# S5 parameter batches of a two-layer encoder: double-buffered tables, fetched two batches ahead on the GpSimd queue

## The chip, the cores and the metric

The kernel runs on one core of a Trainium2 chip. The metric is the device time of one execution in microseconds (us); the time of before is the median of three runs. Engines are named as the profile names them: PE (TensorE), DVE (VectorE), ACT (ScalarE), POOL (GpSimd), SP (SyncE, which here only issues transfers). Each engine works through its own list of instructions in order.

## The reference, cut to what matters

Two layers over 256 tokens of width 2048, all in float32. Layer 0 mixes tokens with sparse latent attention and an RWKV7 recurrence, layer 1 with a complex diagonal state space, S5. Behind each mixer come a cross-attention to a memory and a feed-forward block of width 8192 with squared ReLU.

```python
def s5_mixer(u, lam_re, lam_im, log_dt, b_re, b_im, c_re, c_im, d_skip, w_glu, b_glu):
    ...
    lam_bar = jnp.exp(lam * dt)
    b_bar = ((lam_bar - 1.0) / lam)[..., None] * lax.complex(b_re.astype(f32), b_im.astype(f32))
    c_mat = lax.complex(c_re.astype(f32), c_im.astype(f32))
    ...                       # scan of x <- lam_bar x + b_bar u;  y = Re(C x) + d u, gelu, gate

def squared_relu_mlp(xn, w_up, w_down):
    return jnp.square(jax.nn.relu(xn @ w_up)) @ w_down
```

## The kernel before

Everything is kept transposed, features on partitions and tokens along the free axis. A weight matrix comes in half chunks of [128, 1024] (512 KB): `w_load` (L228) issues the load on SP into a tile `st`, and `w_split` makes of each half of it an exact pair, `whi` (a copy on ACT, L236) and `wlo` (a subtraction on DVE, L238), so that three matmuls (L302 to L304, the third with `wlo`) give the product in full precision. `whi` and `wlo` have a few buffers each: PE runs some quarters of a chunk behind ACT and DVE, and stops when `wlo` is late.

The stage around the change is the feed-forward block of layer 0, `ffn(0, ...)`. It has 64 `up` and 64 `down` units of 48 matmuls each; `mm3` uses four `whi`/`wlo` pairs of 512 columns per unit. After each unit one step of another stream is recorded, `S5Params.steps()`, which prepares layer 1: it turns the parameters of the state space alone into matrices and leaves them in DRAM.

- `base()` makes powers of the state matrix (`pw`), a complex factor `f`, and a table by token, which it stores to the DRAM tile `tokens` (L1333).
- `batch(m)`, m = 0 to 15, has six steps. Step 0 loads `bc` (128 KB, two buffers), `bT` (512 KB) and `tT` (512 KB, from `tokens`), the last two in one buffer each; DVE forms `bb` = `bc`·`f` by `cmul` (six instructions, L1294 to L1299) and ACT copies it into `bd` (L1384, L1385). Step 1: `cmul` of `bT` and `tT` to `bt`. Step 2: `cmul` of `bc` and `pw` to `cl`. Step 3: ACT turns `cl` into `co`; stores `rec2<-co` (L1401) and `rec1<-bt` (L1402). Step 4: 8 small matmuls (L1407) of `bd` and `cl`, copied to `tt`. Step 5: store `rec2<-tt` (L1414).
- `phases()` makes tables `E` on POOL alone: 18 instructions for `u`, then four quarters of 52 instructions, each followed by four stores `rec1<-E` (L1363). All POOL instructions here are recorded at L211, through a wrapper that keeps them in the order in which they are written; `cmul` is shared, so its lines are L1294 to L1299 on DVE. `E` has one buffer, so a quarter begins when the stores of the last one have landed.

`mix1`, after the stage, reads all `rec` tiles back. A scheduler in the tile framework sets the order of each engine's list when the kernel is built; waits follow from the tiles and their buffers. So where an instruction stands in its engine's list is fixed before the kernel runs.

Of the kernel before, what the change touches and what calls it, by code (L numbers as in the profile page):

```python
# [6 lines left out]
F32 = mybir.dt.float32  # L7
# [13 lines left out]
def _tile_weight(w):  # L21
    """[K, M] -> chunks [n, 128, 2048]: per chunk (m-tile, k-tile, column)."""
    K, M = w.shape
    kt, mt = K // P, M // P
    t = w.reshape(kt, P, mt, P).transpose(2, 1, 0, 3)
    per = 2048 // (kt * P)
    t = t.reshape(mt // per, per, P, kt, P).transpose(0, 2, 1, 3, 4)
    return np.ascontiguousarray(t).reshape(mt // per, P, 2048)
# [17 lines left out]
def _consts():  # L46
    """Tables that depend on the shapes alone."""
# [34 lines left out]
def layout(inp):  # L82
# [53 lines left out]
    # features of 8 groups per tile, the channel of a group before the group  # L136
    fo = np.arange(D).reshape(KT, 8, 16).transpose(0, 2, 1).reshape(-1)
    out['win1'] = _tile_weight(inp['odd_w_in'][0][:, fo])
    # past the state space: group bits (1, 0), group bit 2, channel
# [5 lines left out]
    # states on partitions: (group of the pair, state); pairs of groups along the free axis  # L145
# [13 lines left out]
# steps of the streams in the first layer per step of a pair of heads  # L159
# [12 lines left out]
def build(tc, a, parts=('mix0', 'x0', 'f0', 'mix1', 'x1', 'f1')):  # L172
# [5 lines left out]
    with ExitStack() as es:  # L178
# [26 lines left out]
        class InOrder:  # L205
            """An engine whose instructions stay behind all that was issued on it before."""
# [24 lines left out]
        def w_split(st, i, half):  # L231
            """half of a half chunk as an exact pair hi + lo of float32r"""
# [9 lines left out]
        # columns of 512 whose low parts GpSimd takes from VectorE  # L242
# [6 lines left out]
        class Feed:  # L249
            """Half chunks of weights in order, loaded ahead of their use on their own buffers;  # L250
            split ahead of it too, in quarters of a chunk."""
# [23 lines left out]
            def done(self, q=None):  # L275
                """quarter q (the current one) has been used"""
# [5 lines left out]
        class chunk:  # L282
            """1 MiB of weights, split in quarters."""
# [22 lines left out]
        def units(w_ap, xs, evac, kt=16):  # L306
            """All output tiles of a weight; evac(m, psum)."""
# [8 lines left out]
        def mm_k(ps, w, at, x, first, last):  # L316
            """one K tile of an output tile, in three exact float32r products"""
# [6 lines left out]
        def units_g(feed, n, xs, evac, bank, kt=16, grain=4, m0=0, pre=None):  # L324
            """n output tiles of kt products each, a few products per step. pre: steps to take
            between the first products and the first evacuation."""
# [24 lines left out]
        def split(pool_, name, x, scale=None):  # L351
            """x (times a column) as an exact pair of float32r tiles."""
# [10 lines left out]
        def rnorm_g(ring, sq, ind, scale, eps, floor=False):  # L363
            """1/sqrt(scale * sum over a group of features + eps) per token and group,
            as PSUM [128 features, 256 tokens]. The tiles sq hold squares, ind the groups [128, n]."""
# [22 lines left out]
        class Norm:  # L388
            """x * gain, tile by tile, as f32r pairs or in place; 1/rms per token comes later, on the products."""
# [51 lines left out]
        # ---- residual, transposed: [feature, token]  # L441
# [9 lines left out]
        # ---- memory keys and values (do not depend on x)  # L451
# [41 lines left out]
        def soft(sp, nk, bias=None, scale=1.0, ring=tmp):  # L493
            """softmax over the free axis of scores [128, nk]; returns an SBUF tile."""
# [97 lines left out]
        def reduced_sincos(pool_, name, ang, k, y, shape, e=V):  # L592
            """cos and sin of ang, brought to -pi..pi first"""
# [32 lines left out]
        def rope_g(ring, dst, x, cs, perm, rows):  # L626
            """dst = x * cos + (perm x) * sin on the first rows; x in SBUF."""
# [10 lines left out]
        def begin():  # L638
            """Loads x; the first output tiles of the three streams of weights side by side."""
# [22 lines left out]
            def products(i, q):  # L662
                """a quarter of an output tile"""
# [18 lines left out]
        def mix0(nxt):  # L682
# [10 lines left out]
            def load_y(p, y, ys):  # L693
                """mixed heads, back from DRAM and split"""
# [7 lines left out]
            with ExitStack() as right:  # L702
                with ExitStack() as left:
# [7 lines left out]
                    def shifted(pool_, name, ps, i, p0=0, p1=P):  # L711
                        """h + (shift(h) - h) * mu for one tile of features."""
# [43 lines left out]
                    def paced(key, s):  # L756
                        """the steps of a stream that fall to one step of a pair"""
# [41 lines left out]
        class DSA:  # L799
            """Sparse latent attention; everything transposed, [feature, token]."""  # L800
            def __init__(self, n, r0, dp, ya):
# [6 lines left out]
                # the values' tile, free for now, as scratch  # L808
# [792 lines left out]
```

## Time and profile before

| | us |
|---|---|
| median of three runs (lowest, highest) | 2735.43 (2733.37, 2742.15) |
| span of the profiled execution | 2736.0 |
| PE busy | 2608.3 (95%) |
| DVE busy | 1942.3 (71%) |
| ACT busy | 1356.8 (50%) |
| POOL busy | 588.3 (22%) |

The profiled execution has a span of 2736.0 us from its first instruction to its last; no other time of its own is recorded, and it lies 0.6 us above the median of the runs. Busy times overlap, so their sum says nothing; PE is busy nearly always, and what the kernel can win lies in the stretches in which it is not.

### The profile page before, as it was taken

The numbers are of one execution on the slowest core, as the hardware profiler recorded it, in microseconds if no ns is written. First come the engines' busy times: TensorE is split into PE (matmuls) and PEld (weight loads), VectorE is DVE, ScalarE is ACT, GpSimd is POOL, SyncE is SP. The second block draws the span as 40 slices with busy tenths as digits, with TensorE's granted clock in tenths as the row PEclk, the third lists the DMA queues.
The fourth block names the chain that finished last, engine by engine and source line by source line (L and its number), as shares of the span: only waits on it lengthen the run. The fifth ranks groups of instructions, "written<-read, shape, count | busy, mean of one in ns | idle before, by whom it ended". The sixth has DMA issues, their size and how long they took to land.

```text
span 2736.0 us, 57870 instructions
## 1 busy us (share of the span) xinstructions
PE 2608.3 (95%) x22078; PEld 2500.9 (91%) x22078; DVE 1942.3 (71%) x4202; ACT 1356.8 (50%) x2860; POOL 588.3 (22%) x860
## 2 busy tenths in 40 slices
PE   7889999999998999999999998999999999999997
PEld 7877888789898899999999998999999999999997
DVE  6678878757878777777766798566766656666565
ACT  4444445335654455455465545555554454454553
POOL 5344435436686000000000223001400000000001
PEclk9999999899999999999999999999999999999998
DMA  5323344244367777777766586555355555555553
GB/s 195 122 96 112 113 155 153 91 128 168 140 199 250 246 228 235 243 235 230 240 223 242 195 311 232 185 186 190 142 181 183 186 184 185 185 185 186 182 184 136
DMA packets 184038, 510.40 MB, mean 187 GB/s; under 512 B 41808, under 2 KB 66640, under 8 KB 181712
## 3 DMA queue, kind: packets, MB, share of 16 engines
q1 hardware_dynamic: 182704, 504.47, 54.6%
q8 instruction: 173, 2.83, 0.4%
q0 software_dynamic: 768, 2.10, 0.2%
q14 instruction: 105, 0.86, 0.1%
q10 hardware_dynamic: 288, 0.14, 0.0%
HBM read 472.55 MB, written 34.09 MB: 185 GB/s over the span
## 4 chain that ended last, share of the span: by engine, by line
PE 68%; DVE 16%; DMA 8%; issue 4%; ACT 2%; POOL 1%; SPq 0%; DVEq 0%; ACTq 0%; POOLq 0%
PE acc L304 16%; PE acc L302 16%; PE acc L303 16%; DVE wlo L238 5%; PE acc L320 5%; PE acc L321 4%; PE acc L322 4%; DMA tT<-tokens 4%; DMA bc<-s5bc 2%; ACT whi L236 1%; PE ms L1115 1%; DMA st<-up 1%; DMA st<-wA 1%; DVE t L1145 1%; PE ms L1098 1%
## 5 line engine op out<-in xcount | busy, mean ns | idle before, releaser
L238 DVE TENSOR_TENSOR wlo<-st,whi 128x512 fp32r<-128x512 f32 (+3 forms) x1568 | 1058.9, 683 | 541.8 <-ACT whi L236 530.8
L236 ACT CAST whi<-st 128x512 fp32r<-128x512 f32 x1568 | 949.2, 621 | 958.6 <-PE acc L303 462.9
L304 PE MATMUL acc<-hh,wlo 128*128 128x256 f32 x2048 | 582.5, 284 | 16.7 <-DVE wlo L238 16.7
L302 PE MATMUL acc<-hh,whi 128*128 128x256 f32 x2048 | 579.8, 283 | 3.1 <-ACT whi L236 2.5
L303 PE MATMUL acc<-hl,whi 128*128 128x256 f32 x2048 | 578.4, 282 | 0.1
L304 PEld LDWEIGHTS acc<-hh,wlo 128*128 128x128 f32 x2048 | 387.9, 189 | 22.8 <-DVE wlo L238 22.2
L302 PEld LDWEIGHTS acc<-hh,whi 128*128 128x128 f32 x2048 | 387.9, 189 | 5.9 <-ACT whi L236 3.9
L303 PEld LDWEIGHTS acc<-hl,whi 128*128 128x128 f32 x2048 | 387.8, 189 | 0.3 <-DVE hl L357 0.3
L409 POOL TENSOR_TENSOR xnsq<-xnsq,t 128x256 f32<-128x256 f32 x125 | 106.0, 848 | 1105.6 <-PE acc L304 798.3
L240 POOL TENSOR_TENSOR wlo<-st,whi 128x192 fp32r<-128x192 f32 (+2 forms) x274 | 205.7, 758 | 284.5 <-ACT whi L236 216.0
L1438 POOL MEMSET S<- 128x512 f32 x2 | 1.0, 521 | 499.3 <-ACT hh L356 499.3
L304 PE MATMUL acc<-zh,wlo 128*128 128x256 f32 x256 | 72.1, 282 | 0.0
L302 PE MATMUL acc<-zh,whi 128*128 128x256 f32 x256 | 72.0, 281 | 0.0
L303 PE MATMUL acc<-zl,whi 128*128 128x256 f32 x256 | 72.0, 281 | 0.0
L303 PE MATMUL acc<-ol,whi 128*128 128x256 f32 x256 | 71.5, 279 | 0.0
L302 PE MATMUL acc<-oh,whi 128*128 128x256 f32 x256 | 71.5, 279 | 0.0
L304 PE MATMUL acc<-oh,wlo 128*128 128x256 f32 x256 | 71.5, 279 | 0.0
L574 DVE TENSOR_TENSOR t<-acc,xnr 128x256 f32<-128x256 f32 x128 | 53.8, 421 | 20.1 <-PE acc L304 20.1
L356 ACT CAST hh<-t 128x256 fp32r<-128x256 f32 x128 | 51.8, 404 | 32.6 <-DVE t L566 32.2
L357 DVE TENSOR_TENSOR hl<-t,hh 128x256 fp32r<-128x256 f32 x128 | 55.2, 431 | 4.1 <-ACT hh L356 4.1
L575 DVE TENSOR_TENSOR x<-x,t 128x256 f32<-128x256 f32 x128 | 54.3, 424 | 3.6
L566 DVE SCALAR_TENSOR_TENSOR t<-acc,t 128x256 f32<-128x256 f32 x128 | 53.2, 415 | 0.2 <-ACT t L564 0.2
(788 smaller groups left out, 7788.8 us busy)
## 6 DMA issues: line engine op xcount, KB each, us to landing
st<-up SPq DMA_DIRECT2D x256, 512.0 KB, 3.4
st<-down SPq DMA_DIRECT2D x256, 512.0 KB, 3.7
st<-wout SPq DMA_DIRECT2D x64, 512.0 KB, 3.8
st<-wB SPq DMA_DIRECT2D x48, 512.0 KB, 4.0
st<-wkv SPq DMA_DIRECT2D x32, 512.0 KB, 4.0
R<-rec SPq DMA_DIRECT2D x16, 1024.0 KB, 7.5
st<-win SPq DMA_DIRECT2D x32, 512.0 KB, 3.7
st<-glu SPq DMA_DIRECT2D x32, 512.0 KB, 3.7
```

Of the source, the lines that this page charges most:

```text
L236: A.copy(hi, st)
L238: V.tensor_tensor(lo[:, :n], st[:, :n], hi[:, :n].bitcast(F32), OP.subtract)
L240: G.tensor_tensor(lo[:, n:], st[:, n:], hi[:, n:].bitcast(F32), OP.subtract)
L302: T.matmul(ps, hi, xh, start=k == 0, stop=False)
L303: T.matmul(ps, hi, xl, start=False, stop=False)
L304: T.matmul(ps, lo, xh, start=False, stop=k == nk - 1)
L320: T.matmul(ps, hi, xh, start=first, stop=False)
L321: T.matmul(ps, hi, xl, start=False, stop=False)
L322: T.matmul(ps, lo, xh, start=False, stop=last)
L357: V.tensor_tensor(l, x, h.bitcast(F32), OP.subtract)
L409: G.tensor_tensor(self.sq[0], self.sq[0], s, OP.add)
L575: V.tensor_tensor(xT[m], xT[m], t, OP.add)
```

## The change

The three loads of a batch move into `fetch(m)`, all with two buffers. `fetch(0)` and `fetch(1)` are recorded at the end of `base()`, `fetch(m + 2)` in step 2 of `batch(m)`. They are issued by POOL instead of SP, and so are the stores of `tokens`, `co`, `bt` and `tt`. The copies into `bd` are recorded in step 1, after the `cmul` of `bt`. Scratch tiles of `base()` share the buffers of `co`, `bt` and `cl`, since `bT` and `tT` are now taken by the fetches. Comments are gone too, so that lines shift. The arithmetic is as before.

```diff
-                pb = p.tile([P, 2, 64, 8], F32, name='pb')
+                pb = p.tile([P, 2, 64, 8], F32, name='pb', tag='cl')
-                tk = p.tile([P, 1024], F32, name='tT').rearrange('p (m s c g) -> p m s c g', m=16, s=8, c=2)
+                tk = p.tile([P, 1024], F32, name='tk', tag='co').rearrange('p (m s c g) -> p m s c g', m=16, s=8, c=2)
-                tq = p.tile([P, 1024], F32, name='bT').rearrange('p (a q) -> p a q', a=8)
+                tq = p.tile([P, 1024], F32, name='tq', tag='bt').rearrange('p (a q) -> p a q', a=8)
...
-                nc.sync.dma_start(tokens.rearrange('a (r q) -> r a q', r=P), tq)
+                nc.gpsimd.dma_start(tokens.rearrange('a (r q) -> r a q', r=P), tq)
...
+                self.got = {}
+                self.fetch(0)
+                self.fetch(1)
+                yield
+
+            def fetch(self, m):
+
+                if m >= 16:
+                    return
+                p = self.p
+                bc = p.tile([P, 4, 4, 16], F32, name='bc', bufs=2)
+                bT, tT = (p.tile([P, 1024], F32, name=nm, bufs=2) for nm in ('bT', 'tT'))
+                nc.gpsimd.dma_start(bc, a['s5bc'][m])
+                nc.gpsimd.dma_start(bT, a['s5bT'][m].unsqueeze(1).to_broadcast([16, 8, 1024]))
+                nc.gpsimd.dma_start(tT, tokens[m // 2].rearrange('(b s f) -> b s f', b=2, s=8)[m % 2].unsqueeze(0)
+                                    .to_broadcast([16, 8, 1024]))
+                self.got[m] = bc, bT, tT
...
-                bc = p.tile([P, 4, 4, 16], F32, name='bc', bufs=2)
-                nc.sync.dma_start(bc, a['s5bc'][m])
-                bT, tT = (p.tile([P, 1024], F32, name=nm) for nm in ('bT', 'tT'))
-                nc.sync.dma_start(bT, a['s5bT'][m].unsqueeze(1).to_broadcast([16, 8, 1024]))
-                nc.sync.dma_start(tT, tokens[m // 2].rearrange('(b s f) -> b s f', b=2, s=8)[m % 2].unsqueeze(0)
-                                  .to_broadcast([16, 8, 1024]))
+                bc, bT, tT = self.got.pop(m)
...
+                self.cmul((bt[:, :, 0], bt[:, :, 1]), x, y,
+                          t.rearrange('p a b c -> p (a b c)')[:, :512].rearrange('p (g q) -> p g q', g=4))
                 for h in range(2):
                     hs = slice(64 * h, 64 * h + 64)
                     A.copy(bd[hs, 0, :, h], bb[hs, 0])
                     A.activation(bd[hs, 1, :, h], bb[hs, 1], AF.Copy, scale=-1.0)
...
                           (each(self.pw[:, 0, g4], 9), each(self.pw[:, 1, g4], 9)), t)
+                self.fetch(m + 2)
                 yield
...
-                nc.sync.dma_start(rec2[m][:, 0:1024], co.rearrange('p a g o j -> p (a g o j)'))
-                nc.sync.dma_start(rec1[m][:, 0:1024], bt.rearrange('p g a q -> p (g a q)'))
+                nc.gpsimd.dma_start(rec2[m][:, 0:1024], co.rearrange('p a g o j -> p (a g o j)'))
+                nc.gpsimd.dma_start(rec1[m][:, 0:1024], bt.rearrange('p g a q -> p (g a q)'))
...
-                nc.sync.dma_start(rec2[m][:, 1024:2048].rearrange('(i s) (g f) -> g i s f', s=8, g=8),
+                nc.gpsimd.dma_start(rec2[m][:, 1024:2048].rearrange('(i s) (g f) -> g i s f', s=8, g=8),
```

On SP, around batches 6 and 7, each batch of before has six transfers between the weight loads, which are the rows L228 (`up`, `down`):

```order
L1373 DMA tT<-tokens 128x1x1024
L228 DMA st<-up 128x1024 x2
L228 DMA st<-down 128x1024 x4
L1414 DMA rec_5_108<-tt 8x128x128
L228 DMA st<-down 128x1024
L1370 DMA bc<-s5bc 128x256
L1401 DMA rec_6_109<-co 128x1024
L228 DMA st<-down 128x1024 x3
L1372 DMA bT<-s5bT 128x1x1024
L228 DMA st<-down 128x1024
```

After the change SP holds the weight loads of the stage and nothing else, from the first parameter load (`raw`) on:

```order
L228 DMA st<-up 128x1024
L1257 DMA raw<-s5lam 128x192
L228 DMA st<-up 128x1024 x35
L228 DMA st<-down 128x1024 x32
L228 DMA st<-up 128x1024 x32
```

All six transfers have left SP's list.

On POOL, at the beginning of `phases()`, the difference reads as follows; `xnsq` belongs to the norm ahead of the stage, and `ut` and `u` are the first instructions of `phases()`:

```order
 L409 TENSOR_TENSOR xnsq<-xnsq,t 128x256 x8
+L1333 DMA tokens<-tq 128x8x128
+L1350 DMA tT<-tokens 128x1x1024 x2
 L211 TENSOR_TENSOR ut<-scc,scs 128x64
-L211 TENSOR_TENSOR u_11220<-scs,scc 128x64
-L211 TENSOR_TENSOR u_11220<-u_11220,ut 128x64
+L211 TENSOR_TENSOR u_11222<-scs,scc 128x64
+L211 TENSOR_TENSOR u_11222<-u_11222,ut 128x64
```

The whole of `phases()` now stands behind the store of `tokens` and two loads of `tT`, which read what it wrote.

Further down POOL's list, at the end of the second quarter, before the change there are only `E` and its stores (this is the end of the first quarter, and the second ends alike):

```order
L211 TENSOR_TENSOR et<-E 128x16x15
L211 TENSOR_TENSOR E<-E 128x16x15
L211 TENSOR_TENSOR E<-E,et 128x16x15
L1363 DMA rec_0_86<-E 128x2x128
L1363 DMA rec_1_87<-E 128x2x128
L1363 DMA rec_2_88<-E 128x2x128
L1363 DMA rec_3_89<-E 128x2x128
L211 MEMSET E 128x16 x2
```

After it, at the end of the second quarter (the load of `bc` is that of batch 3):

```order
L211 TENSOR_TENSOR et<-E 128x16x15
L211 TENSOR_TENSOR E<-E 128x16x15
L211 TENSOR_TENSOR E<-E,et 128x16x15
L1379 DMA rec_4_90<-E 128x2x128
L1348 DMA bc<-s5bc 128x256
L1379 DMA rec_5_91<-E 128x2x128
L1379 DMA rec_6_92<-E 128x2x128
L1413 DMA rec_1_104<-co 128x1024
L1379 DMA rec_7_93<-E 128x2x128
L1349 DMA bT<-s5bT 128x1x1024
```

From the first `u` to the load of `bc` for batch 3, POOL now has the 18 instructions of `u`, two quarters of 52, and 14 transfers. The loads of `bc` for batches 4 and 5 stand behind 24 and 20 more instructions of `phases()` after the stores of `tt` of batches 1 and 2. The last 16 stand between the loads of batches 5 and 6; behind them POOL's list holds the transfers alone.

On DVE, where a batch gives its `bc` buffer back and the batch after next reads it again, before the change (batch 2 reads bc_12353 for the last time in the first row, and bc_13452 of batch 4 takes that buffer):

```order
L1297 TENSOR_TENSOR t9_12359<-bc_12353,pw_10199 128x576
L238 TENSOR_TENSOR wlo_12387<-st_12384,whi_12386 128x512
L1299 TENSOR_TENSOR cl_12546<-cl_12546,t9_12359 128x576
L574 TENSOR_TENSOR t_12259<-acc_12190,xnr2_10102 128x256
L238 TENSOR_TENSOR wlo_12403<-st_12384,whi_12402 128x512
L575 TENSOR_TENSOR x1_5223<-x1_5223,t_12259 128x256
L1294 TENSOR_TENSOR t9_12917<-bc_12911,f_10113 128x4x16
L238 TENSOR_TENSOR wlo_12421<-st_12418,whi_12420 128x512
L1296 TENSOR_TENSOR bb_12918<-bb_12918,t9_12917 128x64
L1295 TENSOR_TENSOR bb_13459<-bc_13452,f_10113 128x64
```

After it, the same place (bc_11438 of batch 2, bc_12559 of batch 4):

```order
L1297 TENSOR_TENSOR t9_12365<-bc_11438,pw_10199 128x576
L238 TENSOR_TENSOR wlo_12389<-st_12386,whi_12388 128x512
L1299 TENSOR_TENSOR cl_12552<-cl_12552,t9_12365 128x576
L574 TENSOR_TENSOR t_12271<-acc_12202,xnr2_10102 128x256
L238 TENSOR_TENSOR wlo_12405<-st_12386,whi_12404 128x512
L575 TENSOR_TENSOR x1_5223<-x1_5223,t_12271 128x256
L1294 TENSOR_TENSOR t9_12923<-bc_12001,f_10113 128x4x16
L1295 TENSOR_TENSOR bb_13465<-bc_12559,f_10113 128x64
```

The first use of the new `bc` stands 9 rows behind the last read of the old one before, 7 after; over the batches it is 9 or 10 before (but 50 and 32 in the first two), and 7, 10 or 13 after. For `bT` and `tT` the distance grows from 14 to 18 rows to 51 to 68, since each now has two buffers.

## Rows read from the trace of the kernel before

**Rows 1.** The page's head:

```profile
span 2736.0 us, 57870 instructions
```

**Rows 2.** Busy time by stretch: window, length, then each engine's busy us (instructions), PEclk, DMA share, GB/s:

```profile
820.00:1000.00 180.00, 165.16 (x1348) 159.04 (x1347) 139.22 (x257) 84.50 (x186) 47.67 (x86) 0.98 0.78 245
1000.00:1320.00 320.00, 303.31 (x2508) 294.52 (x2507) 231.05 (x456) 161.36 (x364) 0.00 (x0) 0.97 0.75 235
1990.00:2710.00 720.00, 718.11 (x6019) 717.91 (x6018) 440.95 (x767) 361.13 (x661) 8.85 (x12) 1.00 0.52 183
```

**Rows 3.** The same, of line L1407 alone (first PE):

```profile
820.00:1000.00 180.00, 2.67 (x64) 1.59 (x64) 0.98 0.78 245
1000.00:1320.00 320.00, 6.44 (x144) 3.83 (x144) 0.97 0.75 235
```

**Rows 4.** Waits of PE, 820 to 1320: us, times, longest:

```profile
PE acc L304 <- DVE wlo L238: 28.3, 34, 2.5
```

**Rows 5.** Waits of DVE, 820 to 1320:

```profile
DVE wlo L238 <- ACT whi L236: 61.3, 45, 4.5
DVE bb L1295 <- DMA bc<-s5bc: 22.0, 11, 3.1
DVE bt L1295 <- DMA tT<-tokens: 20.5, 7, 4.0
```

**Rows 6.** Waits of ACT, 820 to 1320:

```profile
ACT whi L236 <- DMA st<-down: 83.7, 43, 5.4
ACT bd L1384 <- DVE bb L1299: 24.6, 13, 3.0
```

**Rows 7.** Chain of waits, 1010 to 1062: start, us, what:

```profile
1016.23 6.49 DMA bc<-s5bc
...
1031.72 8.29 DMA tT<-tokens
```

**Rows 8.** The stores of E on POOL, L1363: issue duration, who waited, landing:

```profile
L1363 POOL DMA_DIRECT2D rec<-E x16: 723/723/949, 764.5 to 876.1; - x16
...
  POOL E L211: 12.5, 3
...
DMA to landing us min/median/max: 3.0/4.5/6.0
```

**Rows 9.** Order of time on POOL, 725 to 880: start, us, instruction:

```profile
729.15 0.36 POOL L211 TENSOR_TENSOR ut<-scc,scs 128x64 f32<-128x64 f32 x1 [1.66 <-ACT scc L616]
...
737.87 0.17 POOL L211 MEMSET E<- 128x16 f32 x2
...
764.55 3.12 POOL L1363 DMA_DIRECT2D rec<-E  x4 [0.30 <-POOL E L211]
770.53 0.17 POOL L211 MEMSET E<- 128x16 f32 x2 [2.86 <-DMA rec<-E]
...
802.52 2.93 POOL L1363 DMA_DIRECT2D rec<-E  x4 [0.30 <-POOL E L211]
...
811.32 0.25 POOL L211 TENSOR_TENSOR et<-E 128x16 f32<-128x16 f32 x1
...
816.09 0.71 POOL L211 TENSOR_TENSOR et<-E 128x16 f32<-128x16 f32 x1
```

**Rows 10.** Order of time on SP, 806 to 825:

```profile
808.03 0.43 SPq L1333 DMA_DIRECT2D tokens<-bT  x1
...
815.25 0.59 SPq L1373 DMA_DIRECT2D tT<-tokens  x1
```

**Rows 11.** Order of time on DVE, 820 to 870:

```profile
822.17 0.69 DVE L1294 TENSOR_TENSOR t<-bT,tT 128x512 f32<-128x512 f32 x1 [3.99 <-DMA tT<-tokens]
...
868.65 0.26 DVE L1294 TENSOR_TENSOR t<-bc,f 128x64 f32<-128x64 f32 x1
```

**Rows 12.** Waits of DVE, 868 to 984:

```profile
DVE bt L1295 <- issue: 8.6, 2, 5.1
DVE bb L1295 <- DMA bc<-s5bc: 5.1, 3, 2.7
DVE bt L1295 <- DMA tT<-tokens: 1.9, 1, 1.9
```

More of the change, by code (lines that the diff above doesn't have):

```diff
@@ L1381, in batch @@
                 bd = self.bd[m % 2]
-                for h in range(2):
-                    hs = slice(64 * h, 64 * h + 64)
-                    A.copy(bd[hs, 0, :, h], bb[hs, 0])
-                    A.activation(bd[hs, 1, :, h], bb[hs, 1], AF.Copy, scale=-1.0)
                 over = lambda ap, n: ap.unsqueeze(2).to_broadcast([P, 4, n, 16])
@@ L1392, in batch @@
                           t.rearrange('p a b c -> p (a b c)')[:, :512].rearrange('p (g q) -> p g q', g=4))
+                for h in range(2):
+                    hs = slice(64 * h, 64 * h + 64)
+                    A.copy(bd[hs, 0, :, h], bb[hs, 0])
+                    A.activation(bd[hs, 1, :, h], bb[hs, 1], AF.Copy, scale=-1.0)
                 yield
```

## The prediction

> **What bounds the kernel now.** I began with the page's head [rows 1] and then cut the span into stretches [rows 2], since the change acts only while `ffn(0)` runs beside the batches. The reader should compare matmuls per us. From 1990 to 2710, where the second feed-forward block runs alone, PE does 6019 matmuls in 720 us, 8.36 per us, at a granted clock of 1.00 (the 2.4 GHz level): nothing is missing there. From 820 to 1000 and from 1000 to 1320 it does fewer. What these stretches lose is their length, less their large matmuls at 8.36 per us, less what the batches' own matmuls take [rows 3]. Early: 180 − (1348 − 64)/8.36 − 2.67 = 23.7 us. Late: 320 − (2508 − 144)/8.36 − 6.44 = 30.8 us. So the batches cost 54.5 us beyond their PE work, and that is all a change of theirs can win.
>
> Then the waits, from PE backwards. PE waits on `wlo` of DVE [rows 4]; DVE waits for `whi` of ACT, and for the tables `bc` and `tT` [rows 5]; ACT waits for weight loads, and for `bb` before it can fill `bd` [rows 6]. The chain in the late part shows which of these end last: the landing of `bc` (6.49 us) and of `tT` (8.29) follow each other, with little between them but DVE's own work [rows 7]. These two transfers set the pace, because DVE's list is in order: a `bb` that waits for `bc` holds up the `wlo` behind it, which PE needs. A weight load that stands on SP behind a transfer waiting for a buffer comes late as well.
>
> **The change, late part (1000 to 1320).** `phases()` is over here, before and after. A second buffer puts 51 to 68 DVE instructions between the last read of `tT` and its next load's use, where 14 to 18 stood. At 0.51 us each (231.05 us for 456, rows 2) 51 are 26 us against a landing of 8.3, so the waits on `bT` and `tT` go (20.5 us in rows 5 over both parts). `bc` had two buffers already. Its next load is still issued when `cl` has read the old one, and is used 7, 10 or 13 instructions later, not 9 or 10. This wait stays; only its transfer changes queue. The same size (128 KB) goes over POOL's queue in the stores of `E`, which land in 3.0 to 6.0 us, median 4.5 [rows 8], against the 6.49 of `bc` on SP. I take 4.5; the bounds are 3.0 and, as the slowest like transfer on either queue, 6.5. With 0.7 us for the issue and 7 to 10 instructions at 0.51 in between, 3.6 to 5.1 us, up to 1.6 us of waiting remain per batch (up to 3.6 at 6.5). The buffers of `wlo` absorb a good part: over some eight batches I estimate 5 us lost, with 0 and 14 as bounds. Gain: 30.8 − 5 = 26 us (17 to 31).
>
> Moving the `bd` copies behind `bt` takes ACT's 24.6 us of waiting for `bb` [rows 6] out of the way of `whi`; I cost it at nothing of its own, since it shows on PE through `wlo` and stands in the 30.8. If it did not help, the `whi` half of the loss would remain, which is a rival below. SP's emptied list is counted in the same place. POOL issues what SP did: six issues a batch at 0.72 us [rows 8], 4.3 us in a batch of six units of 48/8.36 = 5.7 us, 34 us in all, on an engine with nothing else to do from 1000 to 1320 [rows 2]. The shared scratch buffers of `base()` cost nothing where PE is fed; `base()` has passed by then.
>
> **The change, early part (820 to 1000).** Here POOL is not free, and its list is in order too. Before, `phases()` starts at 729.15 [rows 9]. Now it stands behind the store of `tokens` and two loads of `tT`, the first of which waited until 815.25 for that store to land [rows 10]; with two issues of 0.72 it begins at 816.7. `bc` of batch 3 stands behind `u` and two quarters. `u` takes 737.87 − 729.15 = 8.7 us. The quarters took 764.55 − 737.87 = 26.7 and 802.52 − 770.53 = 32.0 us next to a busy DVE [rows 9], 0.5 to 0.6 us per instruction; from 811.32 to 816.09, while DVE mostly waited, 12 instructions took 4.77 us, 0.40 each, or 21 us a quarter. DVE will wait for part of the time, so I take 25 a quarter. Fourteen transfers at 0.72 are 10.1, one wait for the single `E` buffer 12.5/3 = 4.2 [rows 8], the landing 4.5:
>
> 816.7 + 8.7 + 50 + 10.1 + 4.2 + 4.5 = 894.2.
>
> DVE forms the first `bb` of batch 3, by its new place in the list, where it ran `bc·f` of batch 2 before, at 868.65 [rows 11]. So it waits about 25 us in all, a part of it already at the `bc` of batch 2, which stands in the same queue. Behind this `bb` are queued all later `wlo`, so ACT, which has no free `whi`, and PE follow. For batches 4 and 5, 24 and 20 instructions of `phases()` at 0.48 are 11.5 and 9.6 us; with issue and landing (5.2) and less 5 us of DVE's work, DVE waits 11 and 10. In place of these 46 us stand now 8.6 + 5.1 + 1.9 = 15.6 [rows 12] (the "issue" wait of `bt` names no releaser; I count it as one for `bT`). The `wlo` buffers absorb some 5. Loss: 46 − 15.6 − 5 = 25. At the lower bound (a landing of 3.0, which counts in `bc` and in the `E` wait, and quarters of 21) the stall is 25 − 8 − 3 = 14 and the loss 10; at the upper (6.0 and 28) it is 38. The first `tT` wait, 3.99 at 822.17 [rows 11], stays, since the same store and load come one behind the other as before. From 729 to 810 DVE is rid of `phases()` beside it; PE is not held by DVE then, so I give this nothing, 2 us at most.
>
> **Sum.** 2736.0 + 25 − 26 = 2735, against the profiled execution, which is 0.6 us above the median; I say 2736. The one unknown with weight is the landing L on POOL's queue. It stands in four `bc` waits and two `E` waits early, and in about four unabsorbed `bc` waits late: ten times in all. So the time is 2736 + 10·(L − 4.5). A measurement of this kernel can tell about 0.3%, 8.2 us, from no change: slower from L = 5.3, faster from 3.7.
>
> **What the Trainium skill says against it.** The stores of `E` beside a DVE busy with tensor_tensor took 0.72 us to issue, 0.95 at most, and landed in 3.0 to 6.0 [rows 8]. "SBUF — State Buffer", section "SBUF: two separate sides", of the Trainium skill warns that a transfer issued from GpSimd has its descriptors written by that engine, and that a VectorE operation on the shared port can hold these up. By the row this costs 0.2 us at the most in an issue, but its landings spread by 3 us, which the rule could explain; by the rule at its worst the result is the slower rival below.
>
> **Rivals.**
> - *Faster*: transfers on POOL's queue land in 3.0 us, the fastest of rows 8, or POOL runs at the 0.40 us pace while DVE waits. For it: DVE waits exactly then. Against it: the median is 4.5 and the transfers crowd (DMA share 0.78). 2736 − 15 = 2721.
> - *`phases()` hurts nobody*: DVE wants `bc` of batch 3 late enough. That needs a quarter in 25/2 = 12.5 us less, or 12.5 us a quarter, below even 21. The late gain alone: 2736 − 26 = 2710.
> - *Slower*: one mechanism, the landing of `bc` on POOL's queue, which is no quicker than the 6.49 of rows 7 once six transfers a batch share that queue. For it: the 6.0 at the top of rows 8. Time: 2736 + 20 = 2756. It decides from L = 5.3.
> - *The change doesn't do what it says*: the queue was not what held up the weights. ACT waits 146 us for weight loads [rows 6] and DVE 61.3 for `whi` against 42.5 for tables [rows 5]. If these follow from how full the transfer engines are (0.75 against 0.52, rows 2), the `whi` share of the late loss stays, 61.3/103.8 = 59%. The late gain is then 0.41 × 26 = 11, and the time 2751.
>
> The last rival rests on the DMA shares of rows 2. "DMA: Bandwidth & Descriptors", section "Issuing engines are not separate DMA queues", of the Trainium skill has this as a rule: transfers run on the same 16 engines whoever issues them, and another issuer saves only its own issuing time. By it the double buffer would still help; by rows 7, where DVE waits for `bc` and `tT` in turn, the latency and not the fullness sets the pace, so I give the rival little.
>
> **Chances.** The forecast (landing near 4.5, within 8.2 us) 0.36; faster with quick landings 0.30, with no early harm 0.03; slower by slow landings 0.22, by full transfer engines 0.09. So faster 0.33, same 0.36, slower 0.31. The likeliest's own range is 2728 to 2744. The range for 8 in 10 goes from 2714, the faster rival with quarters nearer 21 us, to 2757, the slower one.
>
> **What would show each step.** Right: after 1000 no wait on `tT`, waits on `bc` under 2 us, and PE's late loss near 5; `phases()` starting near 817; one DVE wait of some 20 us on `bc` between 840 and 900 with PE idle behind it and its granted clock lower afterwards, then two of about 10. Wrong: `bc` landings far from 4.5 us on POOL's queue, issues much longer than 0.72, quarters far from 25 us, or `whi` still waiting on `st` as long as now in the late part.

## The result, and the profile after

The changed kernel takes 2809.82 us (median of 4 runs, 2800.77 to 2817.95) against 2734.4 for the kernel before in the same comparison. The ratio is 1.0268, 95% interval 1.0233 to 1.0303: 75 us slower, 53 us above the upper end of the predicted range. The profiled execution after has a span of 2816.0 us, that of before 2736.0 [rows 1].

The page of the kernel after, its head and its line on PE:

```profile
span 2816.0 us, 57933 instructions
...
PE 2629.1 (93%) x22078; PEld 2523.9 (90%) x22078; DVE 1939.1 (69%) x4202; ACT 1357.4 (48%) x2860; POOL 636.0 (23%) x957
```

PE runs the same 22078 matmuls but is busy 20.8 us longer (2608.3 before). The rest of the 80 us between the two spans is idle time. Busy time by stretch shows where (columns as in rows 2):

```profile
820.00:1000.00 180.00, 131.99 (x1010) 127.37 (x1008) 111.30 (x199) 63.17 (x136) 115.81 (x248) 0.88 0.63 191
1000.00:1100.00 100.00, 85.31 (x678) 83.30 (x678) 64.89 (x126) 47.37 (x109) 8.10 (x12) 0.91 0.66 208
1100.00:1400.00 300.00, 269.81 (x2195) 263.05 (x2194) 202.95 (x397) 140.57 (x316) 29.64 (x43) 0.94 0.69 218
1400.00:1600.00 200.00, 199.66 (x1699) 198.05 (x1698) 141.42 (x258) 110.11 (x234) 17.36 (x25) 1.00 0.69 226
```

Worked as in the prediction (8.36 matmuls per us; 48, 32, 128 and 48 small ones, 16 a batch in the trace, which take 2.0, 1.3, 5.3 and 2.0 us), these stretches lose 62.9, 21.4, 47.4 and 0.5 us: 132 in place of 54.5, which is 78 of the 80 us. The granted clock is 0.88 to 0.94 where it was 0.97 and 0.98 [rows 2]: in each of these stretches it stood part of the time at the lower of its two levels, 1.2 GHz. It is 1.00 again where PE has no long stops. From 820 to 1400 PE is busy 39 us longer than its matmuls take at 8.36 per us, before it was 23; so 16 of the 20.8 us of longer busy time lie here.

The waits of DVE after, 820 to 1400:

```profile
DVE bt L1295 <- DMA rec<-bt: 92.5, 13, 12.3
DVE bb L1295 <- DMA bc<-s5bc: 61.7, 12, 9.1
DVE wlo L238 <- ACT whi L236: 29.1, 41, 1.8
```

Against rows 5, the wait for `tT` has gone, as forecast. In its place stands a wait that was not there before: the first products of a new `bt` wait for the store of the last one, since `bt` has one buffer. DVE waits 92.5 us in all, 7 us at a time. The waits for `bc` have nearly tripled (22.0 in rows 5). PE's wait on `wlo` follows (28.3 in rows 4):

```profile
PE acc L304 <- DVE wlo L238: 88.2, 28, 11.8
```

One batch in order of time, first POOL, then DVE:

```profile
1160.19 0.53 POOL L1349 DMA_DIRECT2D bT<-s5bT  x1 [8.72 <-DVE t L1297]
1160.72 0.54 POOL L1350 DMA_DIRECT2D tT<-tokens  x1
1162.06 0.56 POOL L1414 DMA_DIRECT2D rec<-bt  x1 [0.80 <-DVE bt L1299]
1185.42 1.30 POOL L1426 DMA_DIRECT2D rec<-tt  x1 [22.80 <-ACT tt L1424]
1189.17 0.57 POOL L1348 DMA_DIRECT2D bc<-s5bc  x1 [2.46 <-DVE t L1297]
```

```profile
1161.09 0.68 DVE L1299 TENSOR_TENSOR bt<-bt,t 128x512 f32<-128x512 f32 x1
...
1170.98 0.69 DVE L1295 TENSOR_TENSOR bt<-bT,tT 128x512 f32<-128x512 f32 x1 [5.34 <-DMA rec<-bt]
...
1196.47 0.23 DVE L1295 TENSOR_TENSOR bb<-bc,f 128x64 f32<-128x64 f32 x1 [4.34 <-DMA bc<-s5bc]
```

`bt` is finished at 1161.77. Its store is issued at 1162.06, behind `bT` and `tT` (1 MB) in the same queue within 2 us. The next batch's first product of `bt`, at 1170.98, stands only 8 rows behind in DVE's list (6 to 9 in nearly all batches; 10 to 15 before). Nothing needs that product so early: its tables were asked for a batch ahead, and the scheduler moved it up. Likewise `bc` is requested 3.75 us behind the store of `tt` (512 KB). What the two transfers take from issue to landing (lines L1414 and L1348):

```profile
L1414 POOL DMA_DIRECT2D rec<-bt x16: 538/559/622, 830.0 to 1447.5; - x16
...
DMA to landing us min/median/max: 3.5/9.3/11.8
```

```profile
L1348 POOL DMA_DIRECT2D bc<-s5bc x16: 567/572/816, 620.5 to 1400.1; - x16
...
DMA to landing us min/median/max: 2.3/7.2/9.4
```

The sixteen loads of `bc` are two groups, the six up to 1000 us and the ten behind it (the same view of the two windows):

```profile
DMA to landing us min/median/max: 2.3/2.6/3.5
```

```profile
DMA to landing us min/median/max: 6.7/7.6/9.4
```

In the second group each load is requested 1.9 to 3.8 us behind the issue of a store of `tt`, which is then still under way; in the first 7.7 us or more behind, or no such store has been issued yet. The store of `bt` shows the same: up to 1380 us it lands in 9.5 us in the median, and in batches 14 and 15, which have no later tables to load ahead of it, in 3.5 and 3.6. On SP, where the trace of before recorded few landings, the one store of `bt` on record landed in 6.8 us, and a `bc` of the late part in 6.49 [rows 7].

### The profile page after: what moved, and what is told of

Its sections match the earlier page's. It is cut to its first block, busy times and chain, and to the rows that moved or that the text cites. A ratio compares the mean times of both kernels' runs of the same rounds, so it can differ in the third digit from the quotient of the medians.

```text
span 2816.0 us, 57933 instructions
## 1 busy us (share of the span) xinstructions
PE 2629.1 (93%) x22078; PEld 2523.9 (90%) x22078; DVE 1939.1 (69%) x4202; ACT 1357.4 (48%) x2860; POOL 636.0 (23%) x957
## 4 chain that ended last, share of the span: by engine, by line
PE 62%; issue 13%; DVE 12%; DMA 6%; POOL 5%; ACT 2%; SPq 0%; DVEq 0%; POOLq 0%; ACTq 0%
PE acc L304 14%; PE acc L302 14%; PE acc L303 14%; PE acc L320 4%; PE acc L321 4%; PE acc L322 4%; DVE wlo L238 3%; DMA bc<-s5bc 2%; POOL E L211 2%; ACT whi L236 1%; PE ms L1115 1%; POOL et L211 1%; DMA st<-down 1%; DVE t L1145 1%; PE ms L1098 1%
## 5 line engine op out<-in xcount | busy, mean ns | idle before, releaser
L302 PE MATMUL acc<-hh,whi 128*128 128x256 f32 x2048 | 586.1, 286 | 0.9 <-ACT whi L236 0.7
L303 PE MATMUL acc<-hl,whi 128*128 128x256 f32 x2048 | 584.5, 285 | 0.1
L304 PEld LDWEIGHTS acc<-hh,wlo 128*128 128x128 f32 x2048 | 394.8, 193 | 64.6 <-DVE wlo L238 64.2
L302 PEld LDWEIGHTS acc<-hh,whi 128*128 128x128 f32 x2048 | 395.0, 193 | 3.3 <-issue 1.6
L303 PEld LDWEIGHTS acc<-hl,whi 128*128 128x128 f32 x2048 | 394.6, 193 | 0.3 <-DVE hl L357 0.3
L1426 POOL DMA_DIRECT2D rec<-tt x16 | 20.9, 1307 | 350.1 <-ACT tt L1424 298.7
L1295 DVE TENSOR_TENSOR bt<-bT,tT 128x512 f32<-128x512 f32 x16 | 11.1, 692 | 104.0 <-DMA rec<-bt 93.7
L304 PE MATMUL acc<-xn8h,wlo 128*128 128x256 f32 x128 | 37.9, 296 | 26.1 <-DVE wlo L238 26.1
```

The source lines that it names most:

```text
L302: T.matmul(ps, hi, xh, start=k == 0, stop=False)
L303: T.matmul(ps, hi, xl, start=False, stop=False)
L304: T.matmul(ps, lo, xh, start=False, stop=k == nk - 1)
```

## The experiments

All ratios are to the kernel before, run on the same chip beside the experiment, with their 95% intervals. Its median was 2729.7 us beside 1 to 4, 2736.2 beside 5 to 8, 2730.0 beside 9 to 12 and 2737.0 beside 13 to 15, so experiments of different groups are best compared by ratio. Theories: **distance** (a table or buffer is wanted again too few DVE instructions after its transfer is issued, so DVE stands for the landing), **queue** (POOL's queue is slow in itself), **buffers** (the second buffers do it), and, from the fourth experiment on, **weights** (late weight loads are a bound of their own).

**1. All transfers back on SP** (`e1_sp`): the seven `nc.gpsimd.dma_start` of the change become `nc.sync.dma_start`.

> The changed kernel with all its S5 transfers put back on SP; two buffers for bT and tT, fetches two batches ahead and the later bd copies stay. Queue theory (the move to POOL's queue costs the time: a store of bt lands there in 9.3 us, not 6.8, and the list of DVE puts the next bt 8 rows behind the last one, not 10 to 14): 2725 to 2745, with waits of bt on the landing of its own store of 30 to 50 us, in place of those on tT. Rival, buffers (the second buffers let the next bt move up into the store of the last one, whatever the queue): 2780 or more.

2712.84 us, ratio 0.9943 (0.9921 to 0.9965). The second buffers with the earlier fetches and the later `bd` copies gain 17 us when the queue is left alone, more than the queue theory expected (2725 or more). DVE's waits, 820 to 1400:

```profile
DVE bb L1295 <- DMA bc<-s5bc: 25.4, 13, 2.9
DVE bt L1295 <- DMA rec<-bt: 19.9, 12, 3.8
```

The wait for `bt`'s store takes the place of that for `tT` here too, but smaller, and below the 30 to 50 us expected: the next `bt` stands 10 to 14 rows behind in nearly all batches, and the landing is 8.0 us (median of three on record).

**2. The queue alone** (`e2_queue_only`): the kernel before, its seven S5 `nc.sync.dma_start` made `nc.gpsimd.dma_start`.

> The kernel before with nothing changed but the queue: its S5 loads and stores are issued by POOL. Queue theory: 2795 to 2825, bt again 8 rows behind the last one and waiting 80 to 100 us in all. Buffers theory: within 10 us of 2735.

2811.99 us, ratio 1.0301 (1.0257 to 1.0345). The whole loss, and a little more, comes with the queue. DVE's waits, 820 to 1400:

```profile
DVE bt L1295 <- DMA rec<-bt: 67.3, 10, 11.1
DVE bb L1295 <- DMA bc<-s5bc: 62.8, 13, 6.7
DVE bt L1295 <- DMA tT<-tokens: 33.4, 4, 12.5
```

The same two waits, and a third on `tT`; that on `bt` is shorter than the 80 to 100 us expected. The list of DVE is again drawn together: 8 rows from one `bt` to the next, so the move acts through the order as well as through the landing (8.5 us in the median). Why the scheduler draws the list tighter when POOL issues the transfers is not shown.

**3. A second buffer for `bt`** (`e3_bt2`; scratch of `base()` shares buffers with `phases()` to make room).

```diff
-                bt = p.tile([P, 4, 2, P], F32, name='bt')
+                bt = p.tile([P, 4, 2, P], F32, name='bt', bufs=2)
```

> The changed kernel with a second buffer for bt as well (small scratch tiles of base() share buffers with tiles of phases() to make room). Theory that the one missing buffer is the cause: the 93.7 us of waits on the store of bt go, 2735 to 2755. Rival, that the scheduler spends any buffer: the first product of bt moves up by a whole batch, and stands 10 to 13 rows behind the last read of the tT whose buffer its own tT takes; with a landing of 8.5 us the wait moves to tT, some 5 us a batch, and the time stays at 2780 to 2815.

2798.07 us, ratio 1.0251 (1.0217 to 1.0286). The rival's price was right and its place wrong: the wait did not move to `tT`; `bt` still waits for a store, 79.2 us in 12 waits. The scheduler moved each `bt` up by a whole batch, so that it stands 8 rows behind the end of the last but one, whose buffer it takes. The buffer was spent on an earlier place in the list, not on slack.

**4. Written order on DVE** (`e4_in_order`): the changed kernel; `VO` keeps an instruction behind all that was recorded on DVE before it.

```diff
+        VO = InOrder(V)
...
-                          (n16(self.f[:, 0, g4]), n16(self.f[:, 1, g4])), t[:, :, 0, :])
+                          (n16(self.f[:, 0, g4]), n16(self.f[:, 1, g4])), t[:, :, 0, :], VO)
...
-                          t.rearrange('p a b c -> p (a b c)')[:, :512].rearrange('p (g q) -> p g q', g=4))
+                          t.rearrange('p a b c -> p (a b c)')[:, :512].rearrange('p (g q) -> p g q', g=4), VO)
```

> The changed kernel with the two cmul of bb and bt on DVE kept in the order in which they are written (46 to 50 rows between one bt and the next, 68 to 71 for bc, in place of 8 and of 7 to 13). Theory of the distance (each table is used too soon behind its request, and no transfer is too slow in itself): waits on bt's store, tT and bc go from 1000 us on, and the time falls below before, to 2690 to 2710. Rival, transfers (the bursts on POOL's queue hold up the weight loads, whose longest landing grew to 13 us of ACT's wait): 2740 or more although those waits are gone.

2737.72 us, ratio 1.0026 (1.0003 to 1.005). The loss of the change is gone, with every transfer still on POOL's queue; but the time does not fall below before. ACT's waits say why (820 to 1400; DVE waits for two stores of `bt`, 14.0 us, and for no other table):

```profile
ACT whi L237 <- DMA st<-down: 115.4, 47, 8.7
ACT whi L237 <- DMA st<-up: 75.1, 29, 6.8
```

Weight loads are waited for in place of the tables (190.5 us together, against 162.0 in the changed kernel), as the rival said, though the time lies 2 us under its 2740.

**5 and 6. Written order with the transfers on SP**, with the second buffers (`e5_sp_in_order`) and in the kernel before without them (`e6_before_in_order`), by the edits of 1 and 4.

> All S5 transfers on SP as in the first experiment, and the cmul of bb and bt kept in written order on DVE as in the fourth. Theory of the distance: the waits on bc (25 us) and on bt's store (20 us) that the first experiment kept go too, and the time falls below its 2713, to 2685 to 2705. Rival, weight loads (as in the fourth experiment DVE's wait for whi grows as the other waits go, because the loads themselves are late): 2710 to 2735.

> The kernel before, with nothing changed but the two cmul of bb and bt kept in written order. Theory of the distance: with one buffer for bT and tT their load is requested a whole batch ahead all the same, so the second buffers are not needed and the time comes within 10 us of the fifth experiment. Rival, buffers: waits on tT or bT remain, 2720 or more, at least 15 us above the fifth.

2721.8 us, ratio 0.994 (0.9922 to 0.9958), and 2735.04 us, ratio 1.0001 (0.9975 to 1.0027). The distance theory fell here as far as it promised a gain: the fifth is where the rival put it, no faster than the first by its ratio. Nor is the sixth within 10 us of the fifth. It lies 13 us above, and not by waits on `tT` or `bT`, so what the second buffers, the earlier fetches and the later `bd` copies are worth here, and through what, stays open. In the sixth DVE waits for no table at all between 820 and 1320; its only large wait, and ACT's for weight loads, are

```profile
DVE wlo L239 <- ACT whi L237: 130.8, 70, 5.7
```

```profile
ACT whi L237 <- DMA st<-down: 93.9, 49, 6.5
ACT whi L237 <- DMA st<-up: 59.8, 30, 6.3
```

and its late part does 2493 matmuls in 320 us where before did 2508 [rows 2]. Taking away the table waits of rows 5 brought nothing. ACT waits for the weights about as long as it did: 153.7 us, against 83.7 [rows 6] and, in the same view,

```profile
ACT whi L236 <- DMA st<-up: 62.6, 30, 4.5
```

But these waits now end last. In the chain of waits from 1010 to 1300 the loads of `bc` and `tT` hold 33% before and weight loads 3%; in the sixth weight loads hold 34%.

**7. `phases()` behind the batches** (`e7_phases_last`): `next(ph, None)` is taken out of the loop over batches, and what is left of `ph` is recorded at its end.

> The changed kernel with phases() recorded behind all 16 batches, so that no instruction of it stands between S5 transfers in POOL's list. Theory of the shared list (bc of batches 3 to 5 late behind phases, and phases behind the store of tt): the loss before 1000 us falls by half, 2775 to 2795. Rival (the early loss is made by bt's store and bc's landing as in the late part, phases add nothing): 2800 or more.

2827.77 us, ratio 1.0328 (1.0292 to 1.0364). The time misses the theory's and lies in the rival's range, but not for the rival's reason: the `E` tables are now late for layer 1 (`E` and `et` of POOL hold 35% of the chain from 1440 to 1640), and PE stops once for 62.7 us. That wait of PE, between 1440 and 1800, and the early stretch, whose loss falls by nearly half, as the theory said:

```profile
PE acc L302 <- ACT whi L236: 62.7, 1, 62.7
```

```profile
820.00:1000.00 180.00, 157.99 (x1255) 152.85 (x1254) 121.96 (x243) 81.85 (x181) 18.91 (x29) 0.93 0.72 227
```

It does 1255 matmuls, not 1010. With 64 small ones (2.67 us) it loses 180 − (1255 − 64)/8.36 − 2.67 = 34.9 us, not 62.9: sharing POOL's list with `phases()` costs 28 us up to 1000.

**8. `bt`'s store ahead of the tables** (`e8_tables_behind_bt`): the loads of `bT` and `tT` are recorded in step 4 and kept in written order on POOL.

> The changed kernel with the loads of bT and tT recorded in step 4 and kept in written order on POOL, so that the store of bt, which stood right behind these 1 MB in POOL's list, stands ahead of them. Theory of the burst: bt's store lands in about 5 us, not 9.3, though the next bt stands 6 rows behind; its waits fall from 93.7 to some 40 us and the time to 2760 to 2785. Rival, the queue is slow in itself: the landing stays at 8 us or more, the time at 2795 or more.

2790.17 us, ratio 1.0199 (1.0165 to 1.0233); the time is 5 us above the theory's, but the landing is as it said, on the same queue beside the same busy DVE (of that store: who waited for it, and its landing):

```profile
  DVE bt L1295: 41.0, 12
...
DMA to landing us min/median/max: 3.0/4.6/8.6
```

The landing halves, from 9.3, and so do the waits. `bT` and `tT` land later in turn, in 7.3 and 9.6 us where it was 5.2 and 8.5. The queue is not slow for this store; it served 1 MB ahead of it. DVE now waits longer for `whi`, 66.7 us and not 29.1, and its waits for `bc` stay at 69.0, so the time falls by less than the wait.

**12. The store of `tt` alone back on SP** (`e12_tt_on_sp`).

> The changed kernel with the store of tt alone back on SP. In POOL's list that store stands right ahead of the load of bc, and waits for ACT with phases() behind it. Theory of the burst: bc lands in 3 to 5 us, not 7.2, and its waits fall from 65 to 30 to 45 us; the time to 2775 to 2795, bt's waits staying near 90 us. Rival, the queue is slow in itself: landing 6.5 or more, time 2800 or more.

2786.23 us, ratio 1.0183 (1.0133 to 1.0234). `bc` lands in 5.4 us, not 7.2, a little above what the theory gave, and its waits fall to 47.4 us: more of the same.

**9, 10, 11. A fourth weight buffer**, beside 5 (`e9_sp_in_order_st4`), 4 (`e10_pool_in_order_st4`) and 1 (`e11_sp_st4`). It exists only while the S5 stage runs; in 9, 10, 11 and 15 small scratch tiles of `base()` share buffers with `phases()`, as in 3, to make room.

```diff
-            st = wst.tile([P, 1024], F32, name='st', tag=f'st{i}')
+            st = (more[0] if i == 3 else wst).tile([P, 1024], F32, name='st', tag=f'st{i}')
...
+        slot4, more = cycle((0, 1, 2, 3)), []
...
-                    self.st = w_load(self.ap[:, j * 512:j * 512 + 1024], self.i)
+                    self.st = w_load(self.ap[:, j * 512:j * 512 + 1024], next(slot4) if more else self.i)
...
+                more.append(self.p)
```

> As the fifth experiment (S5 transfers on SP, bb and bt in written order), with a fourth buffer st for the weight loads of the feed-forward block of layer 0. In the fifth no table was waited for, and ACT waited 184 us for weight loads. Theory of the weights (a load is requested only when one of three buffers comes free, and lands late among the S5 transfers): ACT's wait falls by a third or more and the time to 2685 to 2710. Rival (the transfer engines are full, so that more loads in flight only land later): within 8 us of the fifth, 2714 to 2730.

> As the fourth experiment (S5 transfers on POOL's queue, in written order) with the same fourth buffer. Theory of the weights: 2695 to 2722, at least 15 us under the fourth. Rival, full transfer engines: 2728 or more.

> As the first experiment (S5 transfers on SP, the scheduler's own order) with the fourth buffer. Theory of the weights: the waits on tables of the first (45 us) stay but weights come sooner, 2690 to 2706. Rival (in the scheduler's order the tables bound the kernel, and weights do not): 2708 to 2720.

2693.08, 2697.09 and 2708.11 us; ratios 0.9861 (0.9819 to 0.9903), 0.9874 (0.9831 to 0.9918) and 0.9892 (0.9855 to 0.9928). The ninth and the tenth differ by the queue alone and agree; the tenth is 41 us under the fourth. In the ninth ACT's wait for weights falls from 183.8 to 140.0 us (720 to 1450), a quarter and not the third expected. The eleventh lies 2 us above the theory's range, at the lower edge of the rival's; it decides for neither.

**13, 14, 15. The fourth weight buffer** alone in the kernel before (`e13_before_st4`), with written order in the kernel before (`e14_before_in_order_st4`), and alone in the changed kernel (`e15_after_st4`).

> The kernel before with the fourth weight buffer alone. If the 54 us that the batches cost before are the tables' (the prediction's step), the buffer gains under 8 us: 2727 or more. If they are the weights', it gains as much as in the ninth experiment, 2690 to 2702. If both bound it side by side, so that taking either away alone brings little: 2705 to 2722.

> The kernel before with the fourth weight buffer and bb and bt in written order, single buffers for bT and tT as before. If distance and weights are the two bounds, and second table buffers and the queue are neither, it comes within 10 us of the ninth experiment: 2685 to 2703. If the second table buffers are needed: 2706 or more.

> The changed kernel with the fourth weight buffer alone. If its loss is the stall of DVE on bt's store and bc (both above 5 us at a time, more than split weights can cover), the buffer brings little, 2780 to 2805. If the loss is in the weight loads behind the bursts on POOL's queue (ACT waited up to 13 us for one): 2770 or less.

2721.79 us, ratio 0.9945 (0.9919 to 0.997); 2680.56 us, ratio 0.9788 (0.9766 to 0.981); 2817.82 us, ratio 1.0278 (1.0244 to 1.0311). The fourteenth beats both kernels, and every other experiment by its ratio; it lies 4 us below its expected range and 12 below the ninth, which has the second table buffers besides. Why it beats the ninth stays open. Order alone gave 1.0001 and the buffer alone 0.9945; together they give 2.1%. The thirteenth shows why neither does it by itself (DVE's waits, 820 to 1320):

```profile
DVE bt L1298 <- DMA tT<-tokens: 57.1, 10, 7.3
DVE bb L1298 <- DMA bc<-s5bc: 28.2, 12, 3.1
...
DVE wlo L238 <- ACT whi L236: 8.4, 19, 1.1
```

With the weights early the wait for `whi` falls from 61.3 to 8.4 us, and that for `tT` more than doubles, from 20.5 to 57.1: DVE comes to the same table earlier and stands there longer. With both away, the fourteenth's early and late stretches are

```profile
820.00:1000.00 180.00, 176.90 (x1513) 174.82 (x1513) 146.44 (x275) 99.80 (x218) 37.29 (x68) 0.99 0.80 258
1000.00:1320.00 320.00, 320.00 (x2771) 317.00 (x2770) 255.35 (x499) 180.15 (x390) 0.00 (x0) 1.00 0.81 256
```

Late, (2771 − 144)/8.36 + 6.0 = 320.2 us of work stand in 320: nothing is lost. In the fifteenth, 13 us above its expected range, the buffer brings nothing, since DVE's waits are those of the changed kernel (91.2 us on `bt`'s store, 67.3 on `bc`).

## Why the prediction was wrong

**The bound before: half right.** That the batches cost 54.5 us beyond their own matmuls, and that this is all there is to win, held within a few us: the fourteenth experiment won 56 us and left the late part with no loss and the early part with 5. That the chain's `bc` and `tT` set this pace was wrong. They bound side by side with the weight loads, and the sixth experiment took all of them away for nothing. The `whi` waits of rows 5 (61.3 us) were the larger figure in the same view, and I read them as a consequence. Rows 7 were read rightly, but a chain of waits names only what ends last now, and not what stands close behind it.

**"So the waits on `bT` and `tT` go": the step that failed.** They went, but the same instruction then waited for the next thing on its list. I counted rows between uses of `bT`, `tT` and `bc`, the buffers that the change touches, and not of `bt`, whose single buffer it does not touch but whose store it moves to another queue. That count was to be had beforehand: 10 to 15 rows before, 6 to 9 after, in nearly all batches. The missing term, which the sum puts at nothing without a reason, is 92.5 us of DVE waits. The late part, forecast to lose 5 us, loses some 69 (21.4 + 47.4 + 0.5).

**The landing L: mis-sized.** I took 4.5 us for `bc`, within 3.0 and 6.5; the median was 7.2. By my own rule that makes 2736 + 27 = 2763, the slower rival a step beyond its 6.5. But one L for all was wrong too: the median is 2.6 up to 1000 us and 7.6 behind it, and with four places of the rule in each, its two on `E` left as they were, that makes 2736 − 8 + 12 = 2740. So the landing alone does not carry the miss. Late, I had up to 1.6 us of waiting left per batch, and a good part of it absorbed by the buffers of `wlo`; in the ten batches behind 1000 us DVE waited 45.0 us for `bc`, 4.5 each. The rows I went by (the stores of `E`, rows 8) had nothing but each other ahead of them in their queue. With the store of `tt` moved away `bc` landed in 5.4 us, and with the tables out of its way `bt`'s store landed in 4.6: what was missing was what stands ahead in the same queue.

**The early part: right in kind, 14 us short.** `phases()` began at 812.86, forecast 816.7, and the first `bb` of batch 3 came at 887.02, forecast 894.2, with POOL held up as described (POOL in order of time):

```profile
812.86 0.36 POOL L211 TENSOR_TENSOR ut<-scc,scs 128x64 f32<-128x64 f32 x1
...
883.48 0.59 POOL L1348 DMA_DIRECT2D bc<-s5bc  x1
...
916.06 1.31 POOL L1426 DMA_DIRECT2D rec<-tt  x1 [22.20 <-ACT tt L1424]
```

The loss to 1000 was 62.9 us, forecast 23.7 + 25 = 49. Part of the stall showed on `bt` instead of `bb`, and one item was left out: `phases()` also stands behind the store of `tt`, which waited 22.20 us for ACT. The seventh experiment puts the whole of this sharing at 28 us, close to the forecast's 25. Without the transfers among them the two quarters took 27.6 and 22.5 us, 25 on average as forecast, though one reading behind that figure was loose: from 811.32 to 816.09 DVE did not mostly wait, it was busy for 2.86 of the 4.77 us. In rows 10 it was `bT`, at 814.60, that waited for the store of `tokens`, and `tT` stood behind it.

**The rivals.** Full transfer engines are refuted: the fourteenth moves 256 GB/s at a DMA share of 0.81 in the late part, more than before (235 and 0.75, rows 2), and loses nothing there. The queue as such depends on what else POOL does. The pairs that differ by the queue alone, both in written order, are 4 against 5, ratios 1.0026 and 0.994, and 10 against 9, 0.9874 and 0.9861. The first pair is 0.9% apart by ratio, clear of the intervals (16 us between the medians, 11 between the profiled spans); the second cannot be told apart. In the traces of both pairs the loss stands in the early part, where POOL still has `phases()`; of the first pair, 4 and then 5:

```profile
820.00:1000.00 180.00, 162.58 (x1323) 157.95 (x1322) 129.54 (x237) 82.94 (x187) 127.75 (x235) 0.95 0.71 236
1000.00:1320.00 320.00, 303.38 (x2519) 292.72 (x2519) 229.27 (x449) 160.05 (x359) 33.38 (x49) 0.99 0.71 235
```

```profile
820.00:1000.00 180.00, 168.00 (x1402) 162.36 (x1401) 135.21 (x255) 87.66 (x192) 39.08 (x74) 0.99 0.72 234
1000.00:1320.00 320.00, 303.47 (x2521) 294.26 (x2522) 232.07 (x455) 164.74 (x369) 0.00 (x0) 0.99 0.73 237
```

Early, 79 matmuls fewer are some 9 us of the 11; late the two do the same. In the second pair it is 1378 against 1520 early, and 2706 against 2659 late. So with results not wanted at once the queue costs nothing late; that the early cost is the list shared with `phases()`, as in 7, fits but was not tested in written order. The Trainium skill says in "DMA: Bandwidth & Descriptors", section "Issuing engines are not separate DMA queues", that transfers run on the same 16 engines whichever engine issues them; the late parts of these two pairs agree with it. Without the written order, the same move cost 82 us (2). The other rule, in "SBUF — State Buffer", section "SBUF: two separate sides", that a VectorE operation in a two-port mode can hold up the descriptors of GpSimd's transfers, is not needed here: the 4.6 us of the eighth experiment came beside the same work of DVE, and `bT` landed in 5.2 us from POOL against 5.1 from SP in the fifth (median of five on record).

**What was argued and not shown.** The 82 us of the second experiment act through two things at once, a longer landing (8.5 us for `bt`'s store) and a list drawn 2 to 7 rows tighter; how they share it is not separated. Two runs come near: the eighth halves the landing of `bt`'s store with 6 rows in place of 8, and its waits halve; the fourth leaves the landing at 7.8 us with 46 to 50 rows, and 14.0 us of waits are left. So each takes a good part of that wait away by itself. The `bd` copies were never moved alone, nor were the second buffers given alone.

## What to carry to other kernels

A second buffer gives slack only if the instruction order leaves it: here the scheduler used the second buffer of `bt` to move the next use up, until it stood 8 rows behind the transfer again, and keeping two groups of instructions in written order took away the wait that the buffer had left. Before a transfer is moved to another queue, list what stands ahead of it there and count the rows to the next use of every tile it reads or writes, those of its stores included. When two waits share one engine, taking one away can lengthen the other (here 20.5 to 57.1, and 61.3 to 130.8 us), so a wait's total in the profile is not what its removal is worth: order alone gave nothing, the buffer alone 0.55%, both 2.1%.

## What was not expected of the hardware

Long stops seem to cost twice. In the changed kernel PE is busy 20.8 us longer for the same matmuls, and its granted clock is 0.88 from 820 to 1000, where it stops longest; in the fourteenth experiment PE's busy time is 2580.0 us, 28.3 less than before, at a granted clock of 0.99 and 1.00 in the stretches shown. So a good part of what the stage loses or wins, 28 of the 58 us between the spans 2736.0 and 2677.8, shows as busy time and not as idle time. The clock is a part of it; from 820 to 1000 the sixth experiment shows a granted clock of 1.00 and is still busy 6 us longer than its matmuls take at 8.36 per us, so how much the clock makes is not separated.

The store of `tt` takes POOL 1.30 us to issue where the other transfers of the batches and of `E` take 0.53 to 0.72 in the median; by its shape it moves 1024 pieces of 512 bytes, the stores of `E` 256 pieces.
